# FFN block differences stored with the activations, FFN-out weights split two blocks at a time, four part buffers, and a 31-tap convolution wholly on VectorE

## The chip, the cores and the metric

One core of a Trainium2 chip runs the whole program in one launch. The metric is the device time of that launch in microseconds. TensorE (PE, with its weight loads PEld), VectorE (DVE), ScalarE (ACT), GpSimd (POOL) and SyncE (SP, which issues the DMAs here) run their own instruction streams in order and meet at semaphores.

## The reference, cut to what matters

Two stacks of two layers over one sequence of 1024 tokens of width 1024, in float32. The first stack ("hybrid") mixes four groups of channels; the second has an attention part and a gated FFN of width 2816. What the change touches:

```python
def conformer_conv(u, v, conv_w, conv_b, ln_g, ln_b):      # hybrid, group A: width 31, 256 channels
    h = u * jax.nn.sigmoid(v)
    h = depthwise_conv(h, conv_w) + conv_b
    h = layernorm(h, ln_g, ln_b)
    return jax.nn.silu(h)
...
        u = rmsnorm_2(h, ffn_norm[l])                       # second stack, end of each layer
        h = h + (jax.nn.silu(u @ w_gate[l]) * (u @ w_up[l])) @ w_down[l]
```

## The kernel before, in words

Everything is kept channel-major: a tile holds 128 channels on the partitions and 1024 tokens in the free dimension. Every float32 matmul is done in three passes over operands that are split into a rounded high part and a rest: high weight by high data, high weight by low data, low weight by high data. So each weight piece needs a cast on ACT (`whi`) and a subtraction on POOL (`wlo`, helper `rest`, L193) before PE can use it. The pool `wp` holds three buffers of each; a tile takes whichever of them is free. The order of each engine's stream is not written out by hand: a scheduler places the instructions from a timeline that it keeps itself, so a change of one buffer count can move rows anywhere.

**The convolution.** `conv_a` makes two chunks of 128 channels (tiles `h` and `acc`, pool `cc`) and a list of 60 taps. A tap of chunk 0 is one DVE instruction over 1024 tokens (L695). A tap of chunk 1 is four pairs of 256 tokens: ACT multiplies into `prod` (L699), POOL adds to `acc` (L700). After each of the 16 steps of the sliding-window attention (`swa`: scores on PE, masked minimum on DVE L510, exponential on ACT, reciprocal on DVE L516, scaling on POOL L445, transposes and products on PE) `NTAP0` = 3 taps of the list are emitted, and `NTAP` = 2 after each step of the neighbourhood attention (`na`). The norm of the convolution, `conv_a_norm`, is emitted half way through the second `na` call.

**The FFN, hidden part** (`ffn_hidden`). Gate and up projections are done by a Strassen-Winograd scheme: 7 block products of [128 x 512] outputs in place of 8, with sums and differences of weight blocks made on DVE (`combine`, L1321 to L1324; its first result is the tile `sw`) and of data blocks made ahead. Each index `i` of 22 loads two gate or two up units (`raw`), and PE runs seven blocks of 12 matmuls for it. `leave` turns the sums into activations; the last work of an odd `i` is the finished pair `z` of 128 hidden channels by 1024 tokens twice, which goes to HBM as two tiles `h` (L1351). A pair here is two indices `i`.

**The FFN, output part** (`ffn_out`). Also by seven blocks, for 20 indices `i` (5 groups `g` of four hidden chunks times 4 pairs of output chunks), 42 matmuls each. For every group `hidden_blocks` loads the four chunks back, makes the block differences on DVE (L1417, eight a group) and splits each block (ACT L1202, DVE or POOL L1203). For every index the weights are loaded (`raw`), combined on DVE (L1500 to L1503) and split in seven pieces of 128 x 256 (`wsplit`: ACT L1516, POOL L1517), two pieces to a buffer. The products are added to the residual by DVE straight from PSUM (L1561 to L1582), and those additions free the PSUM banks. The group after next is prepared by `some()`, one step at four places of each index; the first group is prepared at the end of `ffn_hidden`.

## Time and profile before

| what | value |
|---|---|
| median of 3 runs | 3586.26 us (3582.91 to 3586.89) |
| profiled execution: its own time | 3588.15 us |
| its span, first to last instruction | 3586.4 us |
| PE busy | 3390.6 us (95%) |
| DVE busy | 2508.4 us (70%) |
| POOL busy | 2088.5 us (58%) |
| ACT busy | 1570.2 us (44%) |
| mean granted TensorE clock | 0.977 |

The table is an average over stages. By the times of their lines the span divides into: the two hybrid layers up to about 1085 us (in each, the sliding window takes some 120 us); the attention of the first second-stack layer up to about 1530 us, its output projection and first FFN blocks up to 1620 us, its hidden part up to about 2050 us, its FFN output up to 2275 us; then the same for the last layer up to 2790, 2900, 3305 and 3530 us, and the final norm.

### The profile page before, as it was taken

What the parts mean: (1) busy time and instruction counts of PE and PEld (TensorE: products, weight loads), DVE (VectorE), ACT (ScalarE), POOL (GpSimd) and SP (SyncE); (2) the same over time, 40 slices, a digit from 0 to 9 for tenths busy, and PEclk for the clock granted to TensorE, in tenths of its full rate; (3) what the DMA queues carried; (4) which work ended last, traced back from release to release, by engine and by line L of the source; (5) the groups of instructions that cost most, each with busy time, mean ns of one, the idle gap of its engine ahead of it and who ended that gap; (6) DMA issues with size and microseconds to landing.
All of it is one profiled execution on the core that took longest, in us unless ns stands there. A gap on an engine that the chain in (4) does not pass through costs nothing.

```text
span 3586.4 us, 46309 instructions
## 1 busy us (share of the span) xinstructions
PE 3390.6 (95%) x15948; PEld 2785.1 (78%) x15948; DVE 2508.4 (70%) x3963; ACT 1570.2 (44%) x3187; POOL 2088.5 (58%) x1859
## 2 busy tenths in 40 slices
PE   8999999899999999889999989999998899999897
PEld 6788888788888888767777767788887677777676
DVE  6756656755646766686777798766656767667997
ACT  4475442674444554352333333445543523333343
POOL 4785454884573344465666788733334556657884
PEclk9999999999999999999999999999998999999998
DMA  4112532112432223442112243311123422112432
GB/s 130 38 56 54 171 122 75 35 59 75 166 110 87 90 89 123 142 138 83 71 71 74 81 153 106 107 55 52 54 95 132 140 83 71 71 71 83 153 103 80
DMA packets 168956, 336.16 MB, mean 94 GB/s; under 512 B 32432, under 2 KB 43152, under 8 KB 168720
## 3 DMA queue, kind: packets, MB, share of 16 engines
q1 hardware_dynamic: 168720, 333.19, 28.3%
q8 instruction: 126, 2.06, 0.2%
q14 instruction: 110, 0.90, 0.1%
HBM read 253.90 MB, written 76.07 MB: 92 GB/s over the span
## 4 chain that ended last, share of the span: by engine, by line
PE 70%; DVE 13%; POOL 8%; issue 4%; ACT 2%; DMA 2%; SPq 0%; DVEq 0%; POOLq 0%; ACTq 0%
PE pa L221 11%; PE pa L223 11%; PE pa L224 11%; PE pa L1195 3%; PE pa L1192 3%; PE pa L1194 3%; PE po L426 3%; POOL wlo L193 3%; PE T L1195 3%; PE T L1192 2%; PE T L1194 2%; POOL cc L700 2%; PE T L415 2%; PE ps L333 2%; PE ps L334 2%
## 5 line engine op out<-in xcount | busy, mean ns | idle before, releaser
L221 PE MATMUL pa<-xp,whi 128*128 128x512 f32 x2048 | 814.3, 399 | 21.1 <-ACT xp L188 11.9
L223 PE MATMUL pa<-xp,whi 128*128 128x512 f32 x2048 | 815.0, 398 | 6.8 <-DVE xp L189 6.7
L224 PE MATMUL pa<-xp,wlo 128*128 128x512 f32 x2048 | 814.4, 398 | 0.2 <-POOL wlo L193 0.2
L193 POOL TENSOR_TENSOR wlo<-raw,whi 128x512 fp32r<-128x512 f32 x304 | 427.5, 1406 | 480.6 <-ACT whi L204 468.6
L193 POOL TENSOR_TENSOR wlo<-xp,whi 128x512 fp32r<-128x512 f32 x248 | 358.7, 1449 | 193.2 <-ACT whi L1268 192.2
L221 PEld LDWEIGHTS pa<-xp,whi 128*128 128x128 f32 x2048 | 390.1, 191 | 98.3 <-ACT xp L188 12.0
L223 PEld LDWEIGHTS pa<-xp,whi 128*128 128x128 f32 x2048 | 389.9, 190 | 86.0 <-DVE xp L189 10.9
L224 PEld LDWEIGHTS pa<-xp,wlo 128*128 128x128 f32 x2048 | 390.1, 190 | 76.5 <-POOL wlo L193 0.6
L1268 ACT CAST whi<-xp 128x512 fp32r<-128x512 f32 x248 | 153.9, 620 | 409.1 <-PE pa L1194 136.6
L204 ACT CAST whi<-raw 128x512 fp32r<-128x512 f32 x304 | 187.2, 616 | 280.8 <-PE pa L223 171.7
L1192 PE MATMUL pa<-xp,whi 128*128 128x512 f32 x672 | 270.3, 402 | 36.1 <-DVE xp L1576 9.0
L445 POOL TENSOR_SCALAR p<-p,st 128x256 f32<-128x256 f32 (+4 forms) x224 | 156.3, 706 | 225.2 <-DVE st L1038 116.4
L1195 PE MATMUL pa<-xp,wlo 128*128 128x512 f32 x672 | 266.2, 399 | 3.0 <-POOL wlo L193 3.0
L1194 PE MATMUL pa<-xp,whi 128*128 128x512 f32 x672 | 266.4, 396 | 0.0
L700 POOL TENSOR_TENSOR cc<-cc,prod 128x256 f32<-128x256 f32 x240 | 201.0, 858 | 30.0 <-ACT prod L699 23.8
L1192 PEld LDWEIGHTS pa<-xp,whi 128*128 128x128 f32 x672 | 128.7, 191 | 76.3 <-ACT whi L1516 15.9
L419 DVE TENSOR_TENSOR tp<-T,tp 128x512 fp32r<-128x512 f32 (+2 forms) x224 | 131.7, 598 | 68.3 <-ACT tp L418 67.6
L426 PE MATMUL po<-tp,xp 128*128 128x256 f32 (+1 forms) x1024 | 163.1, 279 | 5.9 <-ACT tp L418 5.4
L426 PEld LDWEIGHTS po<-tp,xp 128*128 128x128 f32 x1024 | 148.7, 189 | 24.6 <-ACT tp L418 9.2
L699 ACT ACTIVATE prod<-cc,c 128x256 f32<-128x256 f32 x240 | 119.0, 507 | 109.0 <-POOL cc L700 97.6
L1033 ACT ACTIVATE p<-p,st 128x384 f32<-128x384 f32 (+3 forms) x192 | 117.1, 611 | 108.9 <-DVE st L1026 107.0
L1287 POOL TENSOR_TENSOR xp<-xp,R 128x512 f32<-128x512 f32 x80 | 111.3, 1391 | 86.0 <-DVE xp L1286 86.0
(324 smaller groups left out, 8149.1 us busy)
## 6 DMA issues: line engine op xcount, KB each, us to landing
raw<-w_in SPq DMA_DIRECT2D x208, 256.0 KB, 2.8
xp<-x SPq DMA_DIRECT2D x48, 512.0 KB, 7.4
xp<-w_gate SPq DMA_DIRECT2D x44, 512.0 KB, 4.9
xp<-w_up SPq DMA_DIRECT2D x44, 512.0 KB, 5.3
raw<-w_out SPq DMA_DIRECT2D x80, 256.0 KB, 2.9
x<-xp SPq DMA_DIRECT2D x80, 256.0 KB, 2.0
h<-xp SPq DMA_DIRECT2D x40, 512.0 KB, 2.9
xp<-h SPq DMA_DIRECT2D x80, 256.0 KB, 4.3
```

Source lines behind the costliest of these rows:

```text
L193: self.last_rest = self.nc.gpsimd.tensor_tensor(lo, src, hi.bitcast(F32), ALU.subtract)
L204: nc.scalar.copy(hi, raw)
L221: nc.tensor.matmul(ps[h], hi[:, k - k0, :], x[:, 0, t], start=(k == 0), stop=False)
L223: nc.tensor.matmul(ps[h], hi[:, k - k0, :], x[:, 1, t], start=False, stop=False)
L224: nc.tensor.matmul(ps[h], lo[:, k - k0, :], x[:, 0, t], start=False, stop=(k == nk - 1))
L426: nc.tensor.matmul(O[:, qs[0] * P:qs[0] * P + w], lhsT, pt[part][:, o:o + w], start=((kt, qs) == blocks[0] and i == 0), stop=((kt, qs) == ...
L445: self.nc.gpsimd.tensor_scalar(out, src, colm, 1.0, ALU.mult, ALU.mult)
L700: nc.gpsimd.tensor_tensor(acc[:, i:i + CPW], acc[:, i:i + CPW], q, ALU.add)
L1192: nc.tensor.matmul(ps, hi[:, k, :], xh, start=(start and k == 0), stop=False, skip_group_check=True)
L1194: nc.tensor.matmul(ps, hi[:, k, :], xl, start=False, stop=False, skip_group_check=True)
L1195: nc.tensor.matmul(ps, lo[:, k, :], xh, start=False, stop=(k == len(ops) - 1), skip_group_check=True)
L1268: self.nc.scalar.copy(hi, src)
```

## The change

- `ffn_hidden` writes each of the first ten pairs as seven blocks of 128 x 512 (`BLOCKS`) in place of two tiles of 128 x 1024. Four of the blocks are differences, which DVE makes into a new tile `tq` (one buffer). `hidden_blocks` then loads blocks two at a time and makes no differences. To let two neighbouring chunks be a pair, the order of `w_down_2` is permuted on the host.
- `wsplit` in `ffn_out` splits up to 128 x 512 at a time: four splits an index (three of 512 columns, one of 256) in place of seven of 256. The third and fourth take a whole combined tile.
- The pool `wp` has 4 buffers in place of 3, in the whole program.
- Both chunks of the convolution are DVE taps; `NTAP0` is 1. What is left of the list is emitted after `na` and two gate projections, and `conv_a_norm` after `conv_b`.

```diff
+BLOCKS = ["B11", "T1", "B21", "B22", "T2", "T3", "T4"]
-NTAP0, NTAP = 3, 2
+NTAP0, NTAP = 1, 2
...
-        self.open(es, cp=1, rp=1, wp=3, xp=13, dp=6, sp=8)
+        self.open(es, cp=1, rp=1, wp=4, xp=13, dp=6, sp=8)
...
-                taps[c].append(lambda h=h, acc=acc, t=t, w=self.cwh[:, w0 + t:w0 + t + 1], c=c:
-                               self.tap(h, acc, t, w, c))
+                taps[c].append(lambda h=h, acc=acc, t=t, w=self.cwh[:, w0 + t:w0 + t + 1]:
+                               nc.vector.scalar_tensor_tensor(acc, h[:, t:t + S], w, acc,
+                                                              ALU.mult, ALU.add))
...
-            yd = [self.na(l, w, 0), self.na(l, w, 1, lambda: self.conv_a_norm(l, accs))]
+            yd = [self.na(l, w, 0), self.na(l, w, 1)]
             gc = [self.gate_spill(w, 18 + c) for c in range(2)]
+            self.some_taps(len(self.taps))
             yb = self.conv_b(l, w)
+            self.conv_a_norm(l, accs)
...
             if i % 2:
-                z = Z.pop(i // 2)
+                leave_blocks(i // 2, Z.pop(i // 2))
+
+        def leave_blocks(j, z):
+            if j >= 2 * NSG:
                 for u in range(2):
-                    h = self.tl("dr", (P, S), tag="h", bufs=NH)
+                    h = self.tl("dr", (P, S), tag="h", bufs=FDENSE)
                     nc.sync.dma_start(h, z[:, u, :])
                     hd.append(h)
+                return
+            if j % 2 == 0:
+                hd.append(self.tl("dr", (P, len(BLOCKS), 2, HW), tag="hb", bufs=NSG))
+            d = hd[-1][:, :, j % 2, :]
+            nc.sync.dma_start(d[:, 0, :], z[:, 0, t0])
+            nc.sync.dma_start(d[:, 2:4, :], z[:, 1, :].rearrange("p (b t) -> p b t", b=2))
+            t = self.tl("tq", (P, 4, HW))
+            tt(t[:, 0, :], z[:, 0, t1], z[:, 0, t0], ALU.subtract)
+            tt(t[:, 1, :], z[:, 1, t1], t[:, 0, :], ALU.subtract)
+            tt(t[:, 2, :], z[:, 1, t1], z[:, 0, t1], ALU.subtract)
+            tt(t[:, 3, :], z[:, 1, t0], t[:, 1, :], ALU.subtract)
+            nc.sync.dma_start(d[:, 1, :], t[:, 0, :])
+            nc.sync.dma_start(d[:, 4:7, :], t[:, 1:4, :])
...
+        def load(i):
+            n = min(2, len(BLOCKS) - i)
+            two = self.tl("xp", (P, 2, 2, HW))
+            nc.sync.dma_start(two[:, 0:n], hd[g][:, i:i + n])
...
-            put("T1", k, 2 + k, 0, b11, v, minus(v, b11, b12, b11))
+            put("T1", k, 2 + k, 0, v)
+        steps.append(lambda: load(4))
...
+            m = src.shape[1] // P
+            hi = self.tl("wp", (P, 4, P), F32R, tag="whi")[:, 0:m, :]
+            lo = self.tl("wp", (P, 4, P), F32R, tag="wlo")[:, 0:m, :]
...
-            self.block(A, wsplit(w6), X["T2"], False)
+            w6, w3 = wsplit(r[0])
+            self.block(A, w6, X["T2"], False)
...
-            self.block(A, wsplit(w7), X["T3"], False)
+            w7, w4 = wsplit(r[1])
+            self.block(A, w7, X["T3"], False)
```

**Where the rows of the streams move.** Line numbers of the changed kernel differ: L193 becomes L194, L1287 L1279, L1321 to L1324 become L1313 to L1316, L1340 and L1341 L1332 and L1333, L1345 L1337, L1281 L1273, L230 L231, L1561 to L1582 become L1559 to L1581, and the tap L695 is L686.

First place, the hidden part. POOL before, around the split of `sw` (the first combined weight, for PE's block into T); L1287 is the scaling of activations by the row factor:

```order
L193 TENSOR_TENSOR wlo_18346<-xp_18208,whi_18345 128x512
L193 TENSOR_TENSOR wlo_18372<-xp_18367,whi_18371 128x512
L193 TENSOR_TENSOR wlo_18390<-xp_18367,whi_18389 128x512
L1287 TENSOR_TENSOR xp_18246<-xp_18246,R_15221 128x512
L193 TENSOR_TENSOR wlo_18419<-sw_18406,whi_18418 128x512
L193 TENSOR_TENSOR wlo_18436<-xp_18367,whi_18435 128x512
```

POOL now, at the same point of a pair:

```order
L1279 TENSOR_TENSOR xp_17633<-xp_17633,R_14564 128x512
L194 TENSOR_TENSOR wlo_17759<-xp_17754,whi_17758 128x512
L194 TENSOR_TENSOR wlo_17777<-xp_17754,whi_17776 128x512
L194 TENSOR_TENSOR wlo_17806<-sw_17793,whi_17805 128x512
L1279 TENSOR_TENSOR xp_17633<-xp_17633,R_14564 128x512
L194 TENSOR_TENSOR wlo_17823<-xp_17754,whi_17822 128x512
```

The scaling that stood straight ahead of the split of `sw` now stands behind it.

DVE before, at the end of a pair, from the last weight combination to the first evacuation of the next pair (L230, which reads PE's bank `pa`):

```order
L1324 TENSOR_TENSOR xp_17598<-xp_17598 128x512
L1340 TENSOR_TENSOR dp_17502<-ps_17498,p_3823_17472 128x512
L1341 TENSOR_TENSOR dp_17499<-dp_17499,dp_17502 128x512
L1281 SCALAR_TENSOR_TENSOR xp_17331<-dp_17499,xp_17331 128x512
L1345 TENSOR_TENSOR dp_17502<-dp_17502,T_17575 128x512
L1281 SCALAR_TENSOR_TENSOR xp_17331<-dp_17502,xp_17331 128x512
L230 TENSOR_TENSOR xp_17636<-pa_17601,R_15221 128x512
```

DVE now, the same stretch; `tq` is the tile of differences:

```order
L1316 TENSOR_TENSOR xp_16353<-xp_16353 128x512
L1357 TENSOR_TENSOR tq_16346<-xp_16081 128x512
L1332 TENSOR_TENSOR dp_16252<-ps_16248,p_3465_16222 128x512
L1333 TENSOR_TENSOR dp_16249<-dp_16249,dp_16252 128x512
L1273 SCALAR_TENSOR_TENSOR xp_16081<-dp_16249,xp_16081 128x512
L1337 TENSOR_TENSOR dp_16252<-dp_16252,T_16325 128x512
L1358 TENSOR_TENSOR tq_16346<-xp_16081,tq_16346 128x512
L1359 TENSOR_TENSOR tq_16346<-xp_16081 128x512
L1273 SCALAR_TENSOR_TENSOR xp_16081<-dp_16252,xp_16081 128x512
L1360 TENSOR_TENSOR tq_16346<-xp_16081,tq_16346 128x512
L231 TENSOR_TENSOR xp_16391<-pa_16356,R_14564 128x512
```

Four subtractions have come in, three of them behind the last evacuation of T (L1337) and ahead of the next pair's first.

Second place, the FFN output. DVE before, one index of a middle group, from its first evacuation:

```order
L1561 TENSOR_TENSOR xp_19404<-pa_19884,xp_19404 128x512
L1501 TENSOR_TENSOR raw_19882<-raw_19880,raw_19882 128x256
L1203 TENSOR_TENSOR xp_19851<-xp_19626,xp_19851 128x512
L1576 TENSOR_TENSOR xp_19309<-pa_19788,xp_19309 128x512
L1565 TENSOR_TENSOR xp_19404<-po_19886,xp_19404 128x512
L1417 TENSOR_TENSOR xp_19621<-xp_19621 128x512
L1563 TENSOR_TENSOR xp_19404<-T_19885,xp_19404 128x512
L1568 TENSOR_TENSOR xp_19404<-pa_19884,xp_19404 128x512
L1582 TENSOR_TENSOR xp_19309<-pa_19788,xp_19309 128x512
L1573 TENSOR_TENSOR xp_19404<-T_19885,xp_19404 128x512
L1417 TENSOR_TENSOR xp_19621<-xp_19621 128x512
```

DVE now, from the first evacuation of an index:

```order
L1559 TENSOR_TENSOR xp_18590<-pa_18950,xp_18590 128x512
L1563 TENSOR_TENSOR xp_18590<-po_18952,xp_18590 128x512
L1561 TENSOR_TENSOR xp_18590<-T_18951,xp_18590 128x512
L1581 TENSOR_TENSOR xp_18772<-pa_18862,xp_18772 128x512
L1195 TENSOR_TENSOR xp_19000<-xp_18978,xp_19000 128x512
L1503 TENSOR_TENSOR wr_18944<-dp_19031,wr_18944 128x256
L1567 TENSOR_TENSOR xp_18590<-pa_18950,xp_18590 128x512
L1504 TENSOR_TENSOR wr_18944<-wr_18944 128x256
```

The differences L1417 are gone from between the evacuations; the splits (L1195, before L1203) and combinations stay.

Third place, the sliding window. DVE before, about the fifth step; `cc` is the accumulator of a chunk:

```order
L695 SCALAR_TENSOR_TENSOR cc_777<-cc_710,c_73_275,cc_777 128x1024
L516 RECIPROCAL st_1229<-st_1229 128x2
L695 SCALAR_TENSOR_TENSOR cc_777<-cc_710,c_73_275,cc_777 128x1024
L510 ISA p_1297,st_1299<-ps_1300,c_69_271,c_77_279 128x384
L510 ISA st_1299 128x1
L695 SCALAR_TENSOR_TENSOR cc_777<-cc_710,c_73_275,cc_777 128x1024
L441 TENSOR_TENSOR fold_1086<-po_1061,fold_1086 64x256
```

DVE now, about the fourth step (L511, L517 and L420 are before's L510, L516 and L419, the second half of a split):

```order
L511 ISA st_1099 128x1
L686 SCALAR_TENSOR_TENSOR cc_916<-cc_849,c_73_275,cc_916 128x1024
L420 TENSOR_TENSOR tp_1042<-T_1038,tp_1041 128x256
L686 SCALAR_TENSOR_TENSOR cc_777<-cc_710,c_73_275,cc_777 128x1024
L517 RECIPROCAL st_1099<-st_1099 128x2
L686 SCALAR_TENSOR_TENSOR cc_916<-cc_849,c_73_275,cc_916 128x1024
L231 TENSOR_TENSOR pj_1784<-pa_1785,R_244 128x512
L686 SCALAR_TENSOR_TENSOR cc_777<-cc_710,c_73_275,cc_777 128x1024
L511 ISA p_1140,st_1142<-ps_1143,c_69_271,c_77_279 128x384
```

The taps of both chunks now alternate on DVE, three or four to a step. In both kernels all taps of a layer stand ahead of the first step of `na` on DVE, wherever the program text emits them.

## Rows read from the trace of the kernel before

**Rows 1.** The page, busy time by engine: us, share of the span, instructions.
```profile
PE 3390.6 (95%) x15948; PEld 2785.1 (78%) x15948; DVE 2508.4 (70%) x3963; ACT 1570.2 (44%) x3187; POOL 2088.5 (58%) x1859
```

**Rows 2.** Busy us (x count) by stretch: length, PE, PEld, DVE, ACT, POOL, clock, DMA.
```profile
120.00:240.00 120.00, 109.75 (x553) 91.02 (x552) 80.49 (x162) 78.06 (x187) 106.46 (x120) 0.99 0.13 39
240.00:480.00 240.00, 239.61 (x1278) 203.46 (x1277) 149.30 (x324) 129.75 (x269) 139.16 (x158) 1.00 0.35 107
640.00:760.00 120.00, 111.47 (x562) 93.12 (x561) 76.50 (x161) 83.30 (x201) 108.50 (x128) 0.97 0.14 44
1620.00:2030.00 410.00, 391.17 (x1668) 313.17 (x1667) 290.12 (x319) 128.62 (x217) 255.31 (x179) 0.99 0.22 78
2030.00:2070.00 40.00, 30.30 (x115) 22.63 (x113) 39.06 (x41) 16.02 (x30) 32.56 (x22) 0.87 0.27 96
2070.00:2270.00 200.00, 182.80 (x760) 141.62 (x761) 181.76 (x263) 80.78 (x193) 165.14 (x163) 0.99 0.36 115
2900.00:3285.00 385.00, 366.26 (x1561) 293.09 (x1559) 268.77 (x301) 121.49 (x206) 236.36 (x168) 0.99 0.22 80
3285.00:3325.00 40.00, 31.92 (x121) 23.72 (x120) 39.07 (x38) 15.85 (x30) 33.15 (x22) 0.87 0.25 86
3325.00:3525.00 200.00, 181.55 (x755) 140.83 (x756) 182.68 (x264) 80.65 (x192) 163.97 (x163) 0.99 0.37 117
```

**Rows 3.** Waits of PE, FFN output, 2070 to 2270 us: total, times, longest.
```profile
PE T L1192 <- DVE xp L1563: 5.6, 4, 1.6
PE pa L1192 <- DVE xp L1561: 4.5, 3, 3.1
PE pa L1192 <- DVE xp L1576: 4.5, 4, 1.8
PE pa L1192 <- DVE xp L1568: 2.2, 3, 1.6
```

**Rows 4.** Waits of PE, hidden part, 1620 to 2030 us, then 2900 to 3285 us.
```profile
PE T L1195 <- POOL wlo L193: 16.1, 9, 1.8
...
PE T L1195 <- POOL wlo L193: 16.4, 9, 2.0
```

**Rows 5.** Timeline of one such wait: start, duration, instruction, [idle before it].
```profile
1788.46 0.62 ACT L1268 CAST whi<-sw 128x512 fp32r<-128x512 f32 x1 [1.08 <-PE ps L1194]
...
1789.83 1.68 POOL L1287 TENSOR_TENSOR xp<-xp,R 128x512 f32<-128x512 f32 x1 [1.96 <-DVE xp L1286]
...
1791.47 1.71 POOL L193 TENSOR_TENSOR wlo<-sw,whi 128x512 fp32r<-128x512 f32 x1
...
1793.23 0.50 PE L1195 MATMUL T<-fx,wlo 128*128 128x512 f32 x1 [1.84 <-POOL wlo L193]
```

**Rows 6.** Waits of PE, sliding window, 120 to 240 us.
```profile
PE ps L506 <- DVE st L510: 6.7, 4, 2.9
PE po L426 <- ACT tp L418: 2.5, 2, 1.4
```

**Rows 7.** Instructions of lines 1417 and 695: ns min/median/max, first and last start.
```profile
L1417 DVE TENSOR_TENSOR xp<-xp x80: 671/934/1786, 2042.9 to 3499.3; 128x512 f32<-128x512 f32 x80
...
L695 DVE SCALAR_TENSOR_TENSOR cc<-cc,c,cc x60: 1258/1285/2310, 98.1 to 677.7; 128x1024 f32<-128x1024 f32 x60
```

**Rows 8.** Groups by line, the taps: busy us, mean ns of one, idle before.
```profile
L700 POOL TENSOR_TENSOR cc<-cc,prod 128x256 f32<-128x256 f32 x240 | 201.0, 858 | 30.0 <-ACT prod L699 23.8 <-DVE st L516 4.8 <-DVE tp L419 1.2
...
L695 DVE SCALAR_TENSOR_TENSOR cc<-cc,c,cc 128x1024 f32<-128x1024 f32 x60 | 87.9, 1465 | 0.7
```

**Rows 9.** Waits of DVE, hidden part, 1620 to 2030 us.
```profile
DVE xp L230 <- PE pa L1195: 38.4, 10, 6.5
```

**Rows 10.** Waits of SP's DMA queue, same stretch.
```profile
SPq L1351 <- DVE xp L1281: 322.4, 18, 29.8
```

**Rows 11.** Instructions of line 193, splits of FFN weights: ns min/median/max.
```profile
L193 POOL TENSOR_TENSOR wlo<-xp,whi x248: 1282/1297/1851, 1621.0 to 3310.7; 128x512 fp32r<-128x512 f32 x124
```

More of the change, by code (lines that the diff above doesn't have):

```diff
@@ L557, in na_bias, with na @@
         return t
-    def na(self, l, w, c, between=None):
+    def na(self, l, w, c):
         nc = self.nc
@@ L567, in na @@
         for j in range(2):
-            if j and between is not None:
-                between()
             tb = self.na_bias(l, 2 * c + j)
@@ L1394, in hidden_blocks @@
         v, p = nc.vector, nc.gpsimd
-        def load(k):
-            two = self.tl("xp", (P, 4, HW))
-            for h in range(2):
-                for u in range(2):
-                    f[u, h, k] = two[:, 2 * u + h, :]
-                    nc.sync.dma_start(f[u, h, k], hd[4 * g + 2 * u + k][:, h * HW:(h + 1) * HW])
-        def loads():
-            for k in range(2):
-                load(k)
-        def put(name, k, slot, h, src, eng, sub=None):
+        def load(i):
+            n = min(2, len(BLOCKS) - i)
+            two = self.tl("xp", (P, 2, 2, HW))
+            nc.sync.dma_start(two[:, 0:n], hd[g][:, i:i + n])
+            for j in range(n):
+                for k in range(2):
+                    f[BLOCKS[i + j], k] = two[:, j, k, :]
@@ L1408, in step, with put @@
+        def put(name, k, slot, h, eng):
             def step():
-                if sub is not None:
-                    sub()
                 if slot not in q:
                     q[slot] = self.tl("hx" if g % 2 else "xp", (P, 2, S), F32R)
-                self.put_block(X, name, k, q[slot], h, f[src], eng)
+                self.put_block(X, name, k, q[slot], h, f[name, k], eng)
             steps.append(step)
-        def minus(eng, o, x, y):
-            return lambda: eng.tensor_tensor(f[o], f[x], f[y], ALU.subtract)
+        steps.append(lambda: (load(0), load(2)))
@@ L1434, in hidden_blocks @@
-            put("T4", k, 6, k, b21, p, minus(v, b21, b21, b22))
-        return X, [loads] + steps
+            put("T3", k, 4 + k, 1, p)
+            put("T4", k, 6, k, p)
+        return X, steps
     def dense_ops(self, wd, hd, c0):
@@ L1517, in wsplit @@
             pmark[0] = nc.gpsimd.tensor_tensor(lo, src, hi.bitcast(F32), ALU.subtract)
[L1518 removed]
+            return [(hi[:, k:k + 2, :], lo[:, k:k + 2, :]) for k in range(0, m, 2)]
         def weights(r):
[L1521 to L1522 removed]
+            return wsplit(r[0]), combine(r), r
         def residual(p):
@@ L1760, in layout @@
     a["w_up_2"] = units(i["w_up_2"], NH)
-    a["w_down_2"] = units(i["w_down_2"], KC)
+    wd = units(i["w_down_2"], KC)
+    order = [4 * g + c for g in range(NSG) for c in (0, 2, 1, 3)] + list(range(4 * NSG, NH))
+    a["w_down_2"] = wd[:, :, :, order, :]
     z = np.zeros(RPB_PAD, np.float32)
```

45 lines of the change are left out of this document (11 added, 34 removed).

## The prediction

> **What bounds the kernel now.** I read the busy times first. PE is busy for 3390.6 us and DVE for 2508.4 us of a span of 3586.4 us [rows 1], so the program is a PE program with some 196 us of PE idle time, and a change that removes no matmul can win no more than that. Then I cut the span into stretches, to see where the idle time lies and which engine is full there [rows 2]. PE idle is length less PE busy: 10.3 and 8.5 us in the two sliding windows, 0.4 us in the 240 us behind the first, 18.8 and 18.7 us in the hidden parts, 9.7 and 8.1 us in the 40 us between hidden part and output, 17.2 and 18.5 us in the outputs. Those eight stretches hold 110 us, and they are the ones that the change touches. The reader is to see that a different engine is full in each: POOL in the sliding window (106.5 of 120 us), DVE between the FFN parts (39.1 of 40) and in the output (181.8 of 200), and none in the hidden part (DVE 290 and POOL 255 of 410). Last I read PE's own waits in each, which say whether the full engine is the cause.
>
> **FFN output.** Four groups of waits on DVE's evacuations make 16.8 us of the 17.2 us idle [rows 3]; in the other layer the idle time is 18.5 us [rows 2]. The change takes eight differences L1417 a group out of DVE here, 40 a layer. The last eight fall ahead of the first index, so 32 lie in the 200 us; at the median 0.93 us [rows 7] that is 30 us, and DVE falls from 182 to 152 of 200, with the evacuations no longer queued behind differences. POOL and ACT lose three splits an index but get three of double width; I give that nothing. The gain lies between 0 (if the next full engine, POOL at 165 of 200, just takes DVE's place) and 17 us a layer. DVE is the one named in the waits, so I take two thirds: 11 a layer, **22 us**.
>
> **Between the parts.** DVE has no idle time there (39.1 of 40), and the eight differences of the first group are part of it: 8 x 0.93 to 1.79 us is 7 to 14 us [rows 7], about the size of the hole in PE. The two lots of blocks needed first are now loaded ready to be split. Bounds 0 and 17.8 us for both layers; the DMA must bring seven blocks for what were four tiles, so I take a bit over half, **10 us**. The granted clock is 0.87 here against 0.99 in the hidden part, and a matmul takes 30.30 / 115 = 0.263 us against 391.17 / 1668 = 0.235 [rows 2]: 115 x 0.029 = 3.3 us a layer that a shorter hole can give back. I take half, **3 us**.
>
> **Hidden part, gain.** 16.1 and 16.4 us of PE's idle time are waits for a low weight part before a block into T, 9 each, once per pair [rows 4]. The timeline of one [rows 5] shows how it comes about. The cast of `sw` on ACT waited for PE to leave a buffer (1.08 us, released by a matmul's end); then POOL's split of it had L1287 in front, which itself came late, and ended at 1793.2, 1.84 us after PE wanted it. Four buffers let the cast start one block (some 2.75 us, 12 matmuls of 0.23) earlier, and in the changed POOL stream L1287 stands behind the split of `sw`, not ahead. Bounds 0 and 32.5 us. Both causes of the shown wait are touched, but the changed stream has another narrow place in each pair that the old one did not, so I take two thirds: **22 us**.
>
> **Hidden part, cost.** Ten pairs a layer get four subtractions. At the 0.67 to 0.93 us of L1417 [rows 7] that is 2.7 to 3.7 us a pair of about 41 us. DVE is idle 120 of 410 us, 12 us a pair, of which 3.8 us is the wait at L230 for PE just where three of the four now stand [rows 2, 9]. So the cover is there. Without it all 80 would be on the path, 80 x 0.93 = 74 us. One stands ahead of the evacuation L1340, which frees a PSUM bank. I take **-4 us**, the range is 0 to -74.
>
> SP's queue holds the finished pair's stores until `z` is complete, 322 us of the stretch [rows 10], with the next loads of `w_up` behind. Now the second half of that load stands behind the store of three differences, about one subtraction later, and seven blocks are stored for four. Of PE's waits in the stretch none names a DMA, and the DMA share is 0.22 [rows 2], so I charge nothing; if each pair's late load reached PE, it would be 20 x 0.93 = 19 us.
>
> **Sliding window.** POOL loses 240 additions, 201 us in both layers [rows 8], from an engine that is busy for 106.5 of the 120 us [rows 2], and its scaling step is no longer queued behind them. DVE gets 30 more taps a layer: 30 x 1.285 = 38.6 us [rows 7], and the 30 old ones give back some 5 us, because their mean is now 1.465 us, with POOL adding beside them [rows 8]. DVE is idle for 39.5 of the 120 us [rows 2], and some taps run ahead of the window, so it comes to about 0.9 full. PE waits here for DVE's minimum (6.7 us), and for ACT's cast behind POOL's scaling (2.5 us) [rows 6]. The latter should go, the former may go either way: the loop's POOL leg becomes shorter and its DVE leg longer. Counted in the two PE streams, each of the first eight steps now has 23 to 31 dense matmuls between its scores, before 13 to 25 in seven of the eight, so more PE work covers a longer step. Bounds: all 18.8 us gained, or 2 x 38.6 = 77 us lost. I take half of the idle time, **9 us**. The late norm lies beside 192 residual matmuls, 45 us at the 0.235 us above, and PE is hardly idle in the stretch where taps and norm stand now (0.4 of 240 us [rows 2]): **-2 us** for that and for the wider, later split of `w6`.
>
> **Sum.** 22 + 10 + 3 + 22 - 4 + 9 - 2 = 60 us, from the profiled execution's own 3588.15 us to 3528. That execution was 1.9 us above the median of the runs, so I predict 3527 us, 1.7% faster.
>
> **Rivals.**
> *The wait for the low part stays in the hidden part.* Then the 22 us fall out: 3549 us. For it: POOL is not full there (255 of 410), so the wait is one of order, and the order has only been shuffled. Against it: both waits in front of the split in [rows 5] are touched.
>
> *The moved differences come back as waits.* POOL and DVE slow each other where both read SBUF: L1417 takes 0.67 to 1.79 us [rows 7] and POOL's split 1.28 to 1.85 [rows 11], for the same shapes. If each of the 80 subtractions holds the weight split up by its 0.93 us and half of that reaches PE, 37 us of the gain are lost: 3564 us. For it: the splits were what PE waited for. Against it: POOL has 15 us a pair to spare [rows 2], and the median split takes 1.30 us, near the minimum, so POOL seldom pays. The Trainium skill ("SBUF — State Buffer", section "Who interferes with whom") says that a DVE instruction with two SBUF inputs contends with a GpSimd instruction that reads SBUF, and that the shared ports are an exclusive lock; all four new subtractions and every tap are of that kind. The rows agree on the slowing, but show it mostly on DVE's side; by the rule the sum would be this rival's, by the median of the split it is mine.
>
> *DVE becomes the bound of the sliding window, and the kernel is slower.* The place is the first 13 or so steps, where 60 taps stand between scores, minima and evacuations. If the added 38.6 us a layer all fall on the path, the 9 us gained turn into 77 lost: 3613 us. It decides from the point where DVE's own work with taps takes longer than PE's dense work can cover: 0.9 full by the estimate above. For it: PE's largest wait there is already on DVE. Against it: the taps no longer meet POOL's additions, and PE has more dense work between steps.
>
> *More than I took.* If four fifths of the 110 us go, the clock gives back all of its 6.6 us and nothing is charged, the time is 3588 - 88 - 6.6 - 1.9 = 3492 us. For it: the full engine of three stretches is relieved at once. Against it: PE's idle time in the output outlasts any one wait, with POOL next at 165 of 200.
>
> **Chances.** My sum 0.56, with a range of its own of 3508 to 3545; low-part wait stays 0.14; differences come back 0.12; DVE bound in the window 0.09; more than I took 0.09. A measurement of this kernel can tell about 0.2%, 7 us, from no change. Only the third rival, and the worst of the second, end above 3579 us: slower 0.10, within 0.2% 0.03, faster 0.87. The range that leaves out the third rival and the lower part of the last is 3496 to 3568 us.
>
> **What would show it.** In the changed profile: FFN output with PE idle of 6 to 8 us in 200 and DVE near 0.76 full; the 40 us between the parts shorter and at a higher clock; no wait of a T block for `wlo` in the hidden part, and DVE near 0.79 full; in the sliding window POOL at about a third, taps at about 1.27 us, and PE idle of 5 us or less. The prediction is wrong if PE waits for DVE's minimum or evacuations for tens of microseconds in the sliding window, if a block in the hidden part still waits for `wlo` once per pair, if the loads of `w_up` or of the blocks are named as releasers, or if POOL takes DVE's place in the FFN output.

## The result and the profile after

The changed kernel takes 3541.53 us (median of 4 runs, 3540.17 to 3542.97) against 3585.21 us (4 runs): a ratio of 0.988 with a 95% interval of 0.986 to 0.990, so 44 us or 1.2% faster. 3527 us was forecast. The profiled execution has a span of 3538.3 us, 48.1 less than before, at a mean granted clock of 0.982.

The busy times on the page of the changed kernel, to be read against [rows 1]:

```profile
PE 3372.6 (95%) x15948; PEld 2781.5 (79%) x15948; DVE 2599.0 (73%) x4023; ACT 1444.2 (41%) x2827; POOL 1892.8 (53%) x1499
```

PE has the same 15948 matmuls. DVE gained 90 us of work, POOL and ACT lost 196 and 126 us.

To see where the time went I cut the first second-stack layer at the same events in both traces: from the last score evacuation of the attention to the first evacuation of a `T4` block (entry: output projection, norm, first FFN blocks), to the first evacuation of the FFN output (hidden part), to its last one (output). The first fence shows these three windows of the kernel before, columns as in [rows 2]; the second shows the changed kernel's sliding window and then the same three:

```profile
1469.10:1644.20 175.10, 153.50 (x644) 123.52 (x645) 118.91 (x149) 73.03 (x126) 92.04 (x63) 0.90 0.39 132
1644.20:2069.40 425.20, 397.27 (x1676) 316.08 (x1674) 309.94 (x340) 137.62 (x235) 273.65 (x190) 0.98 0.23 81
2069.40:2293.70 224.30, 206.50 (x863) 161.04 (x864) 199.35 (x290) 91.27 (x214) 178.46 (x177) 0.99 0.36 114
```

```profile
120.00:240.00 120.00, 111.57 (x566) 94.23 (x565) 117.38 (x201) 49.99 (x122) 62.60 (x50) 0.96 0.15 44
...
1465.40:1631.80 166.40, 148.53 (x641) 120.17 (x642) 119.35 (x149) 73.12 (x126) 92.44 (x63) 0.95 0.41 141
1631.80:2053.10 421.30, 395.38 (x1683) 314.70 (x1681) 341.87 (x376) 131.78 (x233) 275.01 (x187) 0.99 0.29 104
2053.10:2266.40 213.30, 202.93 (x854) 160.29 (x854) 172.59 (x252) 82.27 (x155) 153.45 (x119) 0.99 0.44 147
```

In this layer the output gained 11.0 us, the entry 8.7 us and the hidden part, at 425 us by far the longest stretch, only 3.9 us: its PE idle time (length less PE busy) went from 27.9 to 25.9 us, while DVE has 32 us more work there.

The hidden part is best cut once more, at the last but one of its 22 `T4` evacuations. What lies before is the ten pairs whose blocks are stored ("pairs"); what follows, up to the first evacuation of the output, is the last index and the passage to the output ("turn"). Before, then changed:

```profile
1644.20:2038.00 393.80, 374.44 (x1594) 299.31 (x1593) 278.70 (x310) 124.99 (x211) 246.87 (x173) 0.99 0.22 81
2038.00:2069.40 31.40, 22.83 (x84) 16.77 (x82) 31.23 (x32) 12.63 (x24) 26.77 (x18) 0.84 0.24 84
```

```profile
1631.80:2026.50 394.70, 376.30 (x1613) 300.86 (x1612) 317.32 (x350) 120.52 (x211) 251.72 (x173) 1.00 0.28 99
2026.50:2053.10 26.60, 19.07 (x72) 13.84 (x70) 24.55 (x28) 11.26 (x22) 23.29 (x15) 0.91 0.51 176
```

So the pairs gained nothing, and what the hidden part won it won in the turn, 4.8 us; some of that is 12 matmuls (2.8 us at 0.235 us) that now run ahead of the cut. In the turn DVE made the eight differences of the first group (L1417, 2042.9 to 2060.9 us), and PE waited for the evacuation L1336 among them. PE's wait for this evacuation (now L1328), before and changed:

```profile
PE ps L1192 <- DVE dp L1336: 3.7, 1, 3.7
```

```profile
PE ps L1184 <- DVE dp L1328: 0.9, 1, 0.9
```

The waits of PE in the hidden part of the changed kernel, 1620 to 2015 us, answer to [rows 4]:

```profile
PE T L1187 <- POOL wlo L194: 12.9, 8, 1.7
PE pa L1187 <- POOL wlo L194: 2.7, 8, 0.6
```

The sum is as large as the 16.1 us before, but it is not the same wait. Before, it stood at the block `T1`, whose data lie in the pool `fx` and whose weight is `sw` (`T<-fx` in [rows 5]); now it stands at the block `T4` (`T<-xp`), and the wait at `T1` is gone. The idle time ahead of PE's matmuls on `fx`, 1630 to 2030 us, before and changed, then one of the new waits:

```profile
  POOL wlo L193: 14.7, 8
  DVE dp L1336: 0.8, 1
```

```profile
  DVE dp L1328: 0.7, 1
```

```profile
1788.53 0.50 PE L1187 MATMUL T<-xp,wlo 128*128 128x512 f32 x1 [1.59 <-POOL wlo L194]
```

DVE in the hidden part, 1640 to 2040 us, has a wait of a kind that before showed at 0.2 us:

```profile
DVE sw L1313 <- DMA xp<-w_up: 21.7, 9, 3.8
```

PE's waits in 200 us of the output, 2053 to 2253 us, answer to [rows 3]:

```profile
PE pa L1184 <- DVE xp L1559: 6.6, 5, 4.1
PE pa L1184 <- DVE xp L1576: 4.2, 6, 1.2
PE T L1184 <- DVE xp L1561: 2.3, 3, 1.7
```

In the sliding window (120 to 240 us) PE's largest wait has moved from DVE's minimum [rows 6] to POOL's scaling of the scores. The second fence is POOL's own largest wait there:

```profile
PE T L416 <- POOL p L446: 6.2, 3, 4.6
```

```profile
POOL p L446 <- DVE st L517: 24.0, 10, 4.7
```

DVE is busy for 117.4 of the 120 us. The taps as a group on the page:

```profile
L686 DVE SCALAR_TENSOR_TENSOR cc<-cc,c,cc 128x1024 f32<-128x1024 f32 x120 | 168.7, 1417 | 0.7
```

### The profile page after: what moved, and what is told of

It reads as the page before. It is cut to its first block, busy times and chain, and to the rows that moved or that the text cites. A ratio compares the mean times of both kernels' runs of the same rounds, so it can differ in the third digit from the quotient of the medians.

```text
span 3538.3 us, 45687 instructions
## 1 busy us (share of the span) xinstructions
PE 3372.6 (95%) x15948; PEld 2781.5 (79%) x15948; DVE 2599.0 (73%) x4023; ACT 1444.2 (41%) x2827; POOL 1892.8 (53%) x1499
## 4 chain that ended last, share of the span: by engine, by line
PE 58%; DVE 21%; DMA 7%; POOL 6%; issue 6%; ACT 1%; SPq 0%; POOLq 0%; DVEq 0%; ACTq 0%
PE pa L222 10%; PE pa L224 10%; PE pa L225 10%; DVE cc L686 4%; DMA xp<-w_up 3%; PE po L427 3%; PE pa L1184 3%; PE pa L1187 2%; PE pa L1186 2%; POOL wlo L194 2%; PE T L416 2%; PE ps L334 2%; PE ps L335 2%; PE T L1187 1%; DVE dp L1333 1%
## 5 line engine op out<-in xcount | busy, mean ns | idle before, releaser
L194 POOL TENSOR_TENSOR wlo<-raw,whi 128x512 fp32r<-128x512 f32 x304 | 438.4, 1443 | 551.8 <-ACT whi L205 526.9
L222 PEld LDWEIGHTS pa<-xp,whi 128*128 128x128 f32 x2048 | 388.6, 190 | 98.7 <-ACT xp L189 11.6
L194 POOL TENSOR_TENSOR wlo<-xp,whi 128x512 fp32r<-128x512 f32 x248 | 361.0, 1469 | 193.0 <-ACT whi L1260 191.4
L225 PEld LDWEIGHTS pa<-xp,wlo 128*128 128x128 f32 x2048 | 388.7, 190 | 74.8 <-issue 0.2
L446 POOL TENSOR_SCALAR p<-p,st 128x256 f32<-128x256 f32 (+4 forms) x224 | 182.2, 821 | 315.4 <-DVE st L1030 116.5
L420 DVE TENSOR_TENSOR tp<-T,tp 128x512 fp32r<-128x512 f32 (+2 forms) x224 | 132.0, 598 | 53.9 <-ACT tp L419 53.4
L686 DVE SCALAR_TENSOR_TENSOR cc<-cc,c,cc 128x1024 f32<-128x1024 f32 x120 | 168.7, 1417 | 0.7
L1187 PEld LDWEIGHTS pa<-xp,wlo 128*128 128x128 f32 x672 | 127.5, 190 | 44.5 <-POOL wlo L194 17.1
L419 ACT CAST tp<-T 128x512 fp32r<-128x512 f32 (+2 forms) x224 | 110.8, 517 | 106.0 <-PE T L416 82.0
```

Of the source, the lines that this page charges most:

```text
L194: self.last_rest = self.nc.gpsimd.tensor_tensor(lo, src, hi.bitcast(F32), ALU.subtract)
L222: nc.tensor.matmul(ps[h], hi[:, k - k0, :], x[:, 0, t], start=(k == 0), stop=False)
L225: nc.tensor.matmul(ps[h], lo[:, k - k0, :], x[:, 0, t], start=False, stop=(k == nk - 1))
L446: self.nc.gpsimd.tensor_scalar(out, src, colm, 1.0, ALU.mult, ALU.mult)
L686: nc.vector.scalar_tensor_tensor(acc, h[:, t:t + S], w, acc, ALU.mult, ALU.add))
L1187: nc.tensor.matmul(ps, lo[:, k, :], xh, start=False, stop=(k == len(ops) - 1), skip_group_check=True)
```

## The experiments

Two theories stood at first. A: the four part buffers give the gain, and what is lost is that loads of `w_up` stand behind the stores of differences. B: the new instruction order and the wider splits gave the gain, and the subtractions are paid for where they stand now. The later runs refine these. All runs in one table; "us" is the median, the ratio is to runs of the kernel before made beside each run (medians of 3585 to 3587 us), with its 95% interval. Pairs, turn, output: length in the first of the two layers, in us, cut as above; "hidden" is from the first to the last `T4` evacuation. FFN sum: entry, pairs, turn and output, both layers. "wlo" is what PE waited for low parts in 400 us of the hidden part (1630 to 2030), "product" what POOL waited there for DVE ahead of `leave`'s product (L1287, after the change L1279), "w_up" what DVE waited for that load.

| run | us | ratio | hidden | pairs | turn | output | FFN sum | wlo | product | w_up |
|---|---|---|---|---|---|---|---|---|---|---|
| before | 3585.21 | 1 | 424.2 | 393.8 | 31.4 | 224.3 | 1648.4 | 16.1 | 42.6 | 0.2 |
| changed | 3541.53 | 0.988 (0.986 to 0.990) | 417.2 | 394.7 | 26.6 | 213.3 | 1599.5 | 15.9 | 30.3 | 21.7 |
| b_wp4 | 3528.86 | 0.984 (0.982 to 0.985) | 403.1 | 373.2 | 30.5 | 223.3 | 1583.2 | 0.5 | 17.0 | 20.7 |
| a_wp3 | 3609.07 | 1.006 (1.005 to 1.008) | 443.6 | 418.6 | 28.0 | 218.0 | 1672.2 | 24.8 | 52.6 | 29.9 |
| a_nosub | 3524.46 | 0.983 (0.981 to 0.984) | 414.2 | 390.0 | 22.7 | 215.4 | 1586.6 | 15.6 | 47.3 | 14.6 |
| b_wp4_sub | 3555.41 | 0.992 (0.990 to 0.993) | 417.0 | 387.0 | 30.5 | 222.0 | 1609.4 | 10.1 | 23.9 | 31.6 |
| b_wp4_split | 3534.56 | 0.986 (0.984 to 0.987) | 400.7 | 371.3 | 29.9 | 227.5 | 1589.3 | 0 | 22.2 | 20.2 |
| a_late | 3553.39 | 0.991 (0.990 to 0.992) | 428.8 | 403.5 | 27.8 | 209.7 | 1614.8 | 17.8 | 41.4 | 38.1 |
| a_fxz | 3519.20 | 0.982 (0.980 to 0.983) | 408.1 | 384.2 | 21.0 | 218.0 | 1581.2 | 11.6 | 45.4 | 0 |
| b_wp4_fxz | 3532.30 | 0.985 (0.984 to 0.987) | 398.2 | 370.5 | 23.4 | 232.9 | 1585.5 | 2.8 | 22.4 | 0 |
| a_fxz_pool | 3543.13 | 0.988 (0.987 to 0.989) | 419.4 | 395.5 | 21.0 | 222.9 | 1604.4 | 15.8 | 19.9 | 0 |
| a_fxz_defer | 3523.17 | 0.983 (0.981 to 0.984) | 408.1 | 384.1 | 22.1 | 216.5 | 1582.2 | 11.6 | 45.4 | 0 |
| a_conv_old | 3546.42 | 0.988 (0.987 to 0.990) | 421.2 | 397.4 | 26.7 | 213.1 | 1603.0 | 16.2 | 28.7 | 22.3 |
| b_conv | 3585.21 | 0.999 (0.998 to 1.000) | 424.1 | 393.6 | 31.4 | 224.1 | 1649.1 | 16.0 | 43.1 | 0.2 |

(For b_conv the kernel before took 3586.72 us beside it.) The turn takes 30 to 31 us in five of the six kernels that still make the first group's differences there, and 21 to 28 us in all that do not.

**b_wp4: the fourth buffer alone.** The kernel before with

```diff
-        self.open(es, cp=1, rp=1, wp=3, xp=13, dp=6, sp=8)
+        self.open(es, cp=1, rp=1, wp=4, xp=13, dp=6, sp=8)
```

> The kernel before with four part buffers in place of three and nothing else. Theory A (buffers): the fourth buffer gave the 18 us that the changed kernel won between the attention of the second stack and the first T1 block of the hidden part, and it also takes away the 16 us a layer for which PE waits for a low weight part in the hidden part; so about 3585 - 18 - 30 = 3537 us, with the hidden part (first to last evacuation of T4) 424 to about 409 us. Theory B (the differences): the hidden part's wait is one of order and has nothing to do with the buffer count; then only the 18 us go, 3567 us, and the hidden part stays at 424 us.

One number wins 56 us, 13 more than the whole change. That is theory A, with more than it forecast. Its windows for hidden part, pairs alone and output, and PE's wait for a low part before a `T` block (1630 to 2030 us):

```profile
1631.50:2035.20 403.70, 392.49 (x1686) 316.88 (x1684) 317.84 (x339) 133.86 (x234) 276.61 (x190) 0.99 0.24 85
1631.50:2004.70 373.20, 372.50 (x1612) 301.78 (x1611) 287.40 (x310) 121.89 (x211) 252.10 (x174) 1.00 0.23 85
2035.20:2258.50 223.30, 204.43 (x842) 157.77 (x843) 201.32 (x285) 88.36 (x209) 179.74 (x176) 0.98 0.35 112
```

```profile
PE T L1195 <- POOL wlo L193: 0.5, 2, 0.3
```

Length less PE busy falls from 27.9 to 11.2 us in the hidden part, and in the pairs from 19.4 to 0.7 us; the rest is the turn, and the output is as before. The late `w_up` is there too (20.7 us on DVE) and costs PE nothing in this run: a load that is late for DVE need not be late for PE.

**a_wp3: the change without the fourth buffer.** The changed kernel with `wp=3`.

> The changed kernel with three part buffers. Theory A: the entry to the FFN loses its 18 us and the hidden part 10 or more: about 3570 us or above. Theory B: the entry loses 18 us and the hidden part stays at 417 us: about 3560 us. If the buffers did nothing at all: 3541 us.

0.6% slower than before, 39 us above theory A's figure. The hidden part grew by 19 and 16 us, and PE waits longest of all runs for the low part, 23.4 of the 24.8 us at `T1` as before. So without the buffer the rest of the change loses, and it does not take the wait of [rows 4] away.

**a_nosub: the stores without the subtractions.** The changed kernel with the four subtractions left out; the blocks that would be differences are stored from `z` itself. This kernel leaves the differences out of the computation; it only shows what the stores cost in time.

```diff
-            tt(t[:, 0, :], z[:, 0, t1], z[:, 0, t0], ALU.subtract)
...
-            nc.sync.dma_start(d[:, 4:7, :], t[:, 1:4, :])
+            nc.sync.dma_start(d[:, 1, :], z[:, 0, t1])
+            nc.sync.dma_start(d[:, 4:6, :], z[:, 1, :].rearrange("p (b t) -> p b t", b=2))
+            nc.sync.dma_start(d[:, 6, :], z[:, 0, t1])
```

> The changed kernel without the four subtractions a pair: the blocks T1 to T4 are stored from the activations themselves, so this part of the computation is left out; the stores have the same bytes and the same count plus one. Theory A (the load of w_up stands behind the stores in SP's queue and comes late): the load comes only one subtraction earlier, the hidden part goes from 417 to 412 us or stays, in all 3531 to 3541 us. Theory B (the subtractions on DVE and the port shared with POOL hold the hidden part up): the hidden part falls to 405 us or below, in all about 3517 us.

17 us faster than the changed kernel, between the two expectations. The hidden part hardly moved (414 us for 417, A's figure); the pairs gained 4.7 and 6.1 us, the turn 3.9 and 4.0.

**b_wp4_sub: the subtractions without the stores.** b_wp4 with the four subtractions of each pair made into `tq` and used by nobody.

```diff
+                if i // 2 < 2 * NSG:
+                    t = self.tl("tq", (P, 4, HW))
+                    tt(t[:, 0, :], z[:, 0, t1], z[:, 0, t0], ALU.subtract)
...
```

> The kernel before with four part buffers and with the four subtractions of a pair made in the hidden part but neither stored nor used; stores, loads and FFN output as before. Theory A: the hidden part stays near 403 us (up to 406), the kernel at 3529 to 3535 us. Theory B: the hidden part rises to 413 us or above, the kernel to about 3550 us.

Compared over the pairs, where these kernels run 1610 to 1618 matmuls, b_wp4 takes 373 us. The subtractions alone add 14 us a layer, the new stores alone (with the rest of the change) 17 and 15, and both together, in the changed kernel, 21.5 and 21.4: the two add in part. B's bound was met for the subtractions. They do not make the other work longer: in the pairs POOL is busy for 254.4 us in b_wp4_sub and for 252.1 in b_wp4, with 174 instructions each, and DVE's subtractions add 24 us, 0.6 us each. In b_wp4_sub PE waits for a low part again, at `T4` as in the changed kernel, and `w_up` is later still (PE 1630 to 2030, DVE 1640 to 2040 us):

```profile
PE T L1195 <- POOL wlo L193: 9.5, 8, 1.3
```

```profile
DVE sw L1321 <- DMA xp<-w_up: 31.6, 9, 3.9
```

**b_wp4_split: wider splits.** b_wp4 with the changed kernel's `wsplit` in the output, four pieces an index for seven; differences made where they were.

> The kernel before with four part buffers and the FFN-output weights split up to 512 columns at a time; differences are still made in the FFN output. If the 11 us a layer that the changed kernel wins there come from DVE's differences, as the prediction has it: the output stays near 224 us, the kernel near 3529 us. If they come from the wider splits: the output falls to 213 us and the kernel to about 3507 us.

The output gains nothing, 227.5 us after 223.3. So the wider splits alone do not give what the output wins in the changed kernel, which leaves the eight differences a group that left DVE; the moved differences with the old splits were not run.

**a_conv_old and b_conv: the convolution.** The changed kernel with the old convolution, and the kernel before with the new one. The edit of b_conv, cut:

```diff
-NTAP0, NTAP = 3, 2
+NTAP0, NTAP = 1, 2
...
-                               self.tap(h, acc, t, w, c))
+                               nc.vector.scalar_tensor_tensor(acc, h[:, t:t + S], w, acc,
+                                                              ALU.mult, ALU.add))
```

> The changed kernel with the convolution of before (one chunk on ACT and POOL, three taps a step, norm inside the neighbourhood attention). If the convolution change is worth what the two traces show up to the second stack (3.1 us in both layers): about 3545 us. If it is worth the 9 us that the prediction took: 3550 us. If the fourth buffer did those 3 us: 3541 us or below.

> The kernel before with the change to the convolution alone (both chunks' taps as one VectorE operation each, late taps). Theory A (the prediction's term): the sliding-window stretch keeps PE's 4.2 us of waits for the convolution and loses most of the rest, 9 us gained over 120 us, total 3576 us against 3585. Theory B (from the taken-back run, where the old convolution in the changed kernel cost 1 to 5 us): VectorE is full in that stretch now, its exp-free work moves late, and what PE no longer waits for ScalarE and GpSimd it waits for GpSimd's output behind VectorE; gain 1 to 4 us, total 3581 to 3584 us.

By itself the convolution changes nothing that can be measured: 0.999, interval 0.998 to 1.000. Taken back from the changed kernel it costs 5 us, within the 7 us that cannot be told from nothing; 4 of them lie in the first hidden part, which the edit does not touch. The window of 120 to 240 us of b_conv:

```profile
120.00:240.00 120.00, 111.25 (x564) 94.34 (x563) 117.84 (x201) 50.15 (x122) 62.82 (x49) 0.96 0.15 44
```

PE is busy for 1.5 us more than in [rows 2], and DVE is full at 117.8 of 120 us.

**a_late: the store of differences behind the next load.** The changed kernel, the 768 KB store issued after the next `w_up` load.

> The changed kernel, the store of the three late differences issued behind both halves of the next load of w_up. Theory A (the load stands behind the stores): the second half of the load leaves a microsecond or two earlier and no longer shares the engines with 768 KB of stores ahead of it; the hidden part goes from 417 us to 408 us or below, the kernel to about 3524 us. Theory B (the subtractions themselves): it stays at 417 us and 3541 us.

The hidden part got longer, 429 us for 417, which neither theory has. DVE's wait for the load grew, and in SP's queue the load itself (L1285) now waits for the pair's first stores to land (both 1630 to 2030 us):

```profile
DVE sw L1314 <- DMA xp<-w_up: 38.1, 9, 4.4
```

```profile
SPq L1285 <- DMA hb<-xp: 7.0, 7, 1.3
```

The changed kernel has no such wait of the load. So the load wasn't held by its place in SP's queue alone: `w_up` is loaded into a buffer of the pool `xp`, which also holds the pairs `z`, and a pair's buffer is free only when its stores have read it. Why the wait grew as far as it did is not settled by this run.

**a_fxz: a pool of its own for the pairs.** The changed kernel with `z` in pool `fx` (7 buffers there), the first difference made in place in `z`, and `tq` of three blocks.

```diff
-            self.open(es, fx=6, sw=SW, p1=LEAD, tq=1)
+            self.open(es, fx=7, sw=SW, p1=LEAD, tq=1)
...
-                Z[i // 2] = self.tl("xp" if i else "fx", (P, 2, S))
+                Z[i // 2] = self.tl("fx", (P, 2, S))
...
-            tt(t[:, 0, :], z[:, 0, t1], z[:, 0, t0], ALU.subtract)
...
+            tt(z[:, 0, t1], z[:, 0, t1], z[:, 0, t0], ALU.subtract)
```

> The changed kernel with the activation pairs in a pool of their own (one more buffer there), which leaves a buffer of the common pool for the load of w_up; T1 is made in place to pay for it. SP then issues w_up behind the first store of a pair and ahead of the other three. Theory A: the load is early by some 10 us, the waits on it vanish and the hidden part falls to the 403 us of four buffers without the differences, the kernel to about 3513 us. Theory B: the hidden part stays above 410 us, the kernel at 3530 us or above.

This is the fastest kernel of the study: 3519.20 us, 22 below the changed kernel and 10 below b_wp4. DVE waits for no `w_up` any more. The hidden part falls to 408 us, between the two expectations, and PE still waits for low parts. Its windows for hidden part and output:

```profile
1630.00:2035.20 405.20, 390.74 (x1681) 313.98 (x1679) 340.93 (x368) 131.18 (x232) 271.46 (x186) 1.00 0.30 103
2035.20:2253.20 218.00, 205.37 (x858) 161.24 (x859) 176.44 (x259) 82.93 (x155) 154.44 (x121) 0.98 0.45 149
```

One such wait in the timeline of a_fxz, columns as in [rows 5]:

```profile
1735.50 0.63 ACT L1277 ACTIVATE dp<-fx 128x512 f32<-128x512 f32 x1 [4.95 <-DVE fx L231]
...
1736.70 2.39 DVE L1278 SCALAR_TENSOR_TENSOR fx<-dp,fx 128x512 f32<-128x512 f32 x2
...
1736.71 1.83 POOL L194 TENSOR_TENSOR wlo<-xp,whi 128x512 fp32r<-128x512 f32 x1 [1.80 <-ACT whi L1260]
...
1737.83 1.14 ACT L1260 CAST whi<-xp 128x512 fp32r<-128x512 f32 x2
...
1738.51 2.98 POOL L1279 TENSOR_TENSOR fx<-fx,R 128x512 f32<-128x512 f32 x2
...
1740.53 0.39 PE L1184 MATMUL T<-xp,whi 128*128 128x512 f32 x1
...
1741.45 3.75 POOL L194 TENSOR_TENSOR wlo<-xp,whi 128x512 fp32r<-128x512 f32 x3
1742.76 0.50 PE L1187 MATMUL T<-xp,wlo 128*128 128x512 f32 x1 [1.60 <-POOL wlo L194]
```

The casts on ACT were done at 1738.97, but on POOL two products of `leave` (L1279) stood ahead of the low parts, and PE reached `T4` (1740.53) 0.9 us before POOL reached its low part. Unlike in [rows 5], POOL did not wait for DVE ahead of these products: it took them straight behind an earlier split. It had started that split late, after 1.80 us idle for a cast on ACT, which stood behind an activation of `leave` that waited 4.95 us for DVE (L231). The changed kernel shows the same sequence on POOL and PE 45.8 us later in its trace.

**b_wp4_fxz: the early load without differences.** b_wp4 with `z` in `fx`.

> The kernel before with four part buffers and with the pair's product Z in a pool of its own (seven buffers there), so that a w_up load no longer has to wait for the pair's stores; no differences are made. Theory A (the late w_up load costs time only where subtractions push it later): the hidden part stays at 403 us a layer as with four part buffers alone, total 3526 to 3531 us, though VectorE's wait for w_up (20.7 us of it in the stretch with four buffers alone) is gone. Theory B (the load is late even without subtractions and costs PE by itself): the hidden part falls below 400 us, total under 3522 us.

The hidden part fell to 398 us, as B said, and the total did not: 3532 us, as A said. The output takes 233 us, 10 more than in b_wp4, and starts 5 us earlier relative to the hidden part's end. Its window in the output:

```profile
2026.40:2259.30 232.90, 208.71 (x847) 161.57 (x848) 205.46 (x290) 89.58 (x211) 181.72 (x178) 0.96 0.35 112
```

DVE has the same 200 us and more of work there. So a gain in the hidden part is given back where the differences are still to be made; that what arrives earlier waits for DVE there is the likely reason. Against this run the subtractions and stores cost a_fxz 14 us a layer in the pairs, and win 15 in the output.

**a_fxz_pool: the subtractions on GpSimd.** a_fxz with `nc.gpsimd.tensor_tensor` for the four.

> The changed kernel with Z in its own pool (hidden part 408 us, 3519 us) and its four subtractions a pair on GpSimd in place of VectorE. Theory A (what is left of the subtractions' cost, some 5 us a layer, is VectorE's in-order time at the pair's end, which delays the sums that the next split waits for): hidden part 403 to 405 us, total 3509 to 3515 us. Theory B (GpSimd makes every low part in order, and four subtractions of about 1.3 to 1.6 us each stand ahead of the next pair's low parts): the wait of PE for a low part grows, hidden part 412 us or more, total 3527 us or more.

B holds: the hidden part takes 419 us and the total is 24 us above a_fxz. POOL no longer waits long for DVE (19.9 us for 45.4), but is itself late with the low parts.

**a_fxz_defer: the subtractions written later.** a_fxz with the four subtractions emitted behind the next tile's `combine`.

> The changed kernel with Z in its own pool (hidden part 408 us a layer, 3519 us), and the four subtractions of a pair written behind the next tile's weight combinations on VectorE, so that nothing of a pair's differences stands ahead of them. Theory A (what is left of the cost is VectorE's order: at the pair's end the subtractions stand ahead of the combinations from which GpSimd makes the next low part): PE's wait of 10.6 us for the low part in that stretch goes, hidden part 398 to 402 us a layer, total 3498 to 3510 us, as far as the output does not give it back. Theory B (it is VectorE's work as such, wherever it stands, or its sharing of memory with GpSimd): hidden part 406 us or more, total 3515 us or more, and the wait stands at another block.

Nothing moved, because the scheduler put the subtractions back where they had been. DVE in the timeline at the end of one pair, a_fxz first, then a_fxz_defer (whose L1358 is a_fxz's L1357):

```profile
1713.62 0.67 DVE L1337 TENSOR_TENSOR dp<-dp,T 128x512 f32<-128x512 f32 x1
1714.21 1.21 DVE L1357 TENSOR_TENSOR tq<-fx 128x512 f32<-128x512 f32 x1
```

```profile
1715.00 0.68 DVE L1337 TENSOR_TENSOR dp<-dp,T 128x512 f32<-128x512 f32 x1
1715.60 1.21 DVE L1358 TENSOR_TENSOR tq<-fx 128x512 f32<-128x512 f32 x1
```

So neither theory was tested by it.

## Why the prediction was right in sign and 15 us too low

The forecast of faster and the range held; the sum of 60 us was 48 in the profiled execution. That the total came so near is partly luck: the ten pairs of the hidden part, forecast at 18 us gained, brought none, and the entry, which had no term, brought 18. (The last step of the sum is also 1 us off: 3588.15 - 60 - 1.9 is 3526.) Term by term, both layers, from the lengths of the stretches:

- **FFN output, 22 us: right.** 11.0 and 11.5 us a layer. b_wp4_split shows that the wider splits alone do not bring it, which leaves the differences. PE is idle for 10.5 of 200 us, where 6 to 8 were forecast, on the evacuations still, and DVE is 0.82 full, not 0.76.
- **Between the parts, 10 + 3 us: the mechanism was right, the size too large.** The turn gained 4.8 us in each layer, 9.6 in all, of which up to 5.6 are matmuls that moved ahead of the cut; its granted clock rose from 0.84 to 0.91. PE's wait of 3.7 us for the evacuation L1336 among the eight differences fell to 0.9, but PE's idle time there fell only from 8.6 to 7.5 us, because PE now waits 4.1 us for the first evacuation of the output (L1559), with DVE still busy for 24.6 of 26.6 us.
- **Hidden part, gain, 22 us: the mechanism was right, the size too small.** The fourth buffer alone takes away the wait of [rows 4] (16.1 to 0.5 us) and is worth 21 us a layer, 42 in all. In the changed kernel, too, no `T1` block waits for its low part.
- **Entry: no term at all.** My list of "eight stretches" began the hidden part at 1620 us and left out the blocks ahead. The change gains 8.7 and 9.4 us there, b_wp4 as much or more (9.7 and 13.1) and a_wp3 only 0.4 and 2.5, so it is the buffer. Of the first layer's 8.7 us, 3.7 are PE idle time, and the other 5 are a shorter PE busy time for about as many matmuls (641 for 644), with the granted clock at 0.95 after 0.90 (the last section has its rows).
- **Hidden part, cost, 4 us: this is the step that failed.** "So the cover is there" was read from DVE's mean idle time, 12 us a pair. Measured against b_wp4 over the pairs it is 21.5 us a layer, 43 in all, as much as the buffer gains. The subtractions alone, with the old stores, cost 28 us. That is near the 37 us of the rival in which the moved differences come back as waits, and they do come back as waits for weight splits; but the rival had them come through longer splits, and POOL's busy time in the pairs is the same (251.7 us in the changed kernel, 252.1 in b_wp4). It is also why the changed profile looks as if the low-part rival had come true: one edit removed the wait at `T1`, and another brought one of much the same size at `T4`. The prediction had cut its gain for "another narrow place in each pair"; this may be it.
- **SP's queue, nothing charged: wrong in part.** Late `w_up` loads are named as releasers of DVE (21.7 us), which I had written down as a sign of being wrong. Moving the load ahead of a store in the queue made it worse (a_late), giving the pairs a pool of their own took it away. a_fxz, with the late load removed, is 10 us a layer shorter in the pairs; without differences the same step gives 2 to 3 (b_wp4 to b_wp4_fxz).
- **Sliding window, 9 us: oversized.** POOL fell to half (62.6 of 120 us; a third was forecast), and DVE filled to 0.98 instead of 0.9; the taps take 1.417 us in the mean, not 1.27. PE's wait went from DVE's minimum to POOL's scaling, which waits for DVE. Up to the first attention of the second stack the span is 3.1 us shorter, 2.6 in b_wp4 with the old convolution, and b_conv cannot be told from no change.
- **Late norm and wider split, -2 us:** what remains (attention, turn between the layers, end) is 4 us longer.

The sum from the two profiled executions: 22.5 (output) + 9.6 (turn) - 1.4 (pairs) + 18.1 (entry) + 3.1 (hybrid layers) - 3.9 (the rest) = 48.0 us.

The Trainium skill ("SBUF — State Buffer", "Who interferes with whom") says that a DVE instruction with two SBUF inputs contends with a GpSimd instruction that reads SBUF. The trace agrees as far as that such subtractions take unequal times: 0.67 to 1.77 us in a_fxz, as L1417 did. As far as busy times show it, this is not what the moved differences cost: in the pairs of b_wp4_sub POOL is busy 2.3 us longer than in those of b_wp4, while the stretch is 14 us longer, and a_nosub, with no subtractions at all, still pays 15 to 17 us a layer.

What stays open is why the stores alone bring a low-part wait back, and by which path the subtractions do. In most runs PE's wait for low parts goes with POOL's wait for DVE ahead of the product: 17.0 to 22.4 us in the three runs with 0 to 2.8 us of PE wait, 29 to 53 us in most of those with 11 us or more. b_wp4_sub (23.9) and a_fxz_pool (19.9, where POOL subtracts itself) are the exceptions. That POOL has `leave`'s products ahead of the low parts is not enough by itself. In b_wp4 two of them stand straight ahead of the low part of `T4` as well, and PE loses nothing, because POOL comes to that low part before PE comes to the block:

```profile
1775.71 2.94 POOL L1287 TENSOR_TENSOR xp<-xp,R 128x512 f32<-128x512 f32 x2 [0.63 <-DVE xp L1286]
1778.60 2.54 POOL L193 TENSOR_TENSOR wlo<-xp,whi 128x512 fp32r<-128x512 f32 x2
```

```profile
1778.84 0.39 PE L1192 MATMUL T<-xp,whi 128*128 128x512 f32 x1
...
1779.95 0.50 PE L1195 MATMUL T<-xp,wlo 128*128 128x512 f32 x1
```

POOL is 0.2 us early there and 0.9 us late in the changed kernel and a_fxz, so about a microsecond decided in the pairs shown. An order fixed by hand, with the low part ahead of the products, which would show what that microsecond is worth, was not tried.

## What to carry to other kernels

Mean idle time of an engine is no cover for new work on it: look at which in-order queues stand behind the place where the work goes, and run that one part alone. Cut the trace so that a wait and what causes it fall into the same stretch: at the last `T4` evacuation the passage to the output seemed to lose 3 us a layer, and at the one before it gains 5. When several edits come together, take each back by itself; here a single buffer count was worth more than the whole (56 us for 44), and an edit that lost time was hidden behind it. When a store moves later, ask which loads need the buffer that it frees.

## What the runs showed that I had not expected

With the same subtractions and stores, taking the pairs out of the shared pool was worth 22 us, and a third of what was gained ahead of the output came back as a longer output (pairs and turn 16 and 15 us shorter in the two layers, output 5 and 7 longer). And the entry's gain is half clock. The window of 1580 to 1620 us, where the attention's norm ends and the first FFN blocks begin, of the kernel before and then of the changed one (the same times, with the changed kernel 4 to 12 us further in its work):

```profile
1580.00:1620.00 40.00, 26.55 (x94) 20.29 (x93) 34.15 (x35) 18.33 (x33) 25.16 (x16) 0.74 0.35 118
```

```profile
1580.00:1620.00 40.00, 32.22 (x131) 25.16 (x130) 36.33 (x37) 19.04 (x35) 30.72 (x20) 0.91 0.36 118
```

PE is idle for 13.5 us there before and for 7.8 after, and the mean granted clock, which mixes time at 2.4 and at 1.2 GHz, is 0.74 before and 0.91 after: 0.282 us of PE time a matmul before, 0.246 after.
